# A 4096 matmul by Strassen's products on one core: the first product of five regions taken in quarters as well

## The chip, the cores and the metric

The kernel runs on one core of a Trainium2 chip. The metric is device time in microseconds (us). The kernel before took 1525.79 us (median of 3 runs, 1524.71 to 1526.01).

A core has a matrix engine (TensorE, "PE" in the profile, with its weight loads as "PEld"), a vector engine (VectorE, "DVE"), a scalar engine (ScalarE, "ACT"), GpSimd ("POOL") and a queueing engine (SyncE, "SP"). Each runs its own list of instructions in the order in which the program issued them, and waits where an operand is not there yet or a buffer is not free. TensorE accumulates into PSUM, eight banks of 128 x 512 float32. DMAs are issued from the lists of SP, ACT and POOL.

## The reference

```python
def reference(a, b, alpha):          # a, b: 4096 x 4096 float32, alpha = 0.01
    x = np.matmul(a, b)
    return np.where(x > 0, x, alpha * x)
```

## The kernel before

**Regions and products.** The output is cut into 4 row groups g of 1024 rows and 4 pairs j of 1024 columns: 16 regions (g, j). A region's output is a 2 x 2 block matrix of 512 x 512 blocks, and it is computed by Strassen's scheme in Winograd's form: seven block products instead of eight. A = (a11 a12; a21 a22) and B = (b11 b12; b21 b22) are the halves of the group's rows and the pair's columns, split along the inner dimension of 4096 into 2048 + 2048. Of A come the sums s1 = a21 + a22, s2 = s1 - a11, s3 = a11 - a21, s4 = a12 - s2; of B the sums t3 = b22 - b12, t2 = t3 + b11, t1 = b22 - t2 (the code writes it over t2) and t4 = b21 - t2. `PRODUCTS` names the order: 0 is a11 b11, 1 is a12 b21, 2 is s2 t2, 3 is s3 t3, 4 is s1 t1, 5 is a22 t4, 6 is s4 b22. In the regular regions the order of the work is 0, 1, 2, then "fifth" (s1 t1), "fourth" (s3 t3), "sixth" (a22 t4) and "seventh" (s4 b22). Everything is float16 in SBUF; whether that is allowed for the given numbers is judged at the end from measurements of squares (`Measure`, `judge`); another path stands ready if not.

**Whole products and quarters.** A whole product is 64 matmuls of 512 columns (two inner halves k, 8 chunks c, 4 row tiles mt), issued in `product` at line 831, one bank for each row tile. A product "in quarters" applies the seven-product scheme once more to the 512 x 512 blocks: seven quarter products of 16 matmuls of 256 columns (`quarter_product`, line 770), from quarter sums of both operands. In a "chain" one bank collects three of them, and ScalarE copies the running sum into other banks as their seed at the right moment.

**Which regions do what.** The first region (0, 0) has its own code; the other 15 are the loop over `regions`. In group 0 all products are whole. In groups 1 to 3 the order of pairs is 2, 0, 3, 1 (in group 3: 2, 0, 1, 3). The first of a group (pair 2) has products 0 to 4 whole and sixth and seventh in quarters. The last of groups 1 and 2 is "turning": it loads the next group's rows, and only its fourth product is in quarters. The other seven are regular (`in_fourth`): products 0, 1, 2 whole, the other four in quarters. The set `FIFTH` holds just these seven.

**Buffers.** Banks 0 to 3 and 4 to 7 change places as `y` and `z` from region to region. Product 0 ends in `y`, is copied to `z` (line 1132) as the seed of product 1, and stays in `y` as that of product 2. The results wait in tiles `c` (two pools, `side` and `1 - side`, two tiles each); `leave` applies the leaky factor (line 313, VectorE) and stores them (line 1076, SP), a store for each row tile. Quarter sums live in three buffers `a16` and in a tile `x` of four quarters (`t`). Those of S1, of a22 and of s4 are made once a group and kept in DRAM (`kept_q`), from where each region loads them (`load_sums`, line 762). s2 is kept in DRAM too and loaded anew in each region (`load_s2`).

**B.** Blocks of B come through POOL's queue, which casts them to float16 (line 547). Pair 2 of group 0 leaves a float16 copy in DRAM, pair 2 of group 1 its t3 and t2 (`kept_t`), which groups 2 and 3 load in place of b12 and the sums. Pairs 0, 1 and 3 leave b21 and b22 (`kept_half`, loaded at line 544).

**Order on VectorE in a regular region.** The seventh product's adds (lines 1005, 1009, 1011) and two leaky passes; in the second region of a group s3's second and S1's quarter sums (line 719); t3 and t2 for both k (line 603); a measurement if one is due (`EARLY`, `MEASURED`; its squares are ScalarE's, line 231); the leaky passes of product 1; t4 = b21 - t2 for both k; t1 for the first k, a quarter sum of t3 (line 696); t1 for the second k in two column halves (line 1225), which wait for the end of product 2, since they overwrite t2; then the quarter sums of the fifth product (lines 696 to 706).

Of the kernel before, what the change touches and what calls it, by code (L numbers as in the profile page):

```python
# [8 lines left out]
P = 128  # L9
# [28 lines left out]
OTHERS = (0, 3)  # L38

# [9 lines left out]
def kernel(  # L49
# [149 lines left out]

    def plain(t):  # L200
        return t.rearrange("p c m e -> p (c m e)").rearrange("p (c m) -> p c m", c=KC)
# [14 lines left out]
    class Measure:  # L216
# [21 lines left out]
        def end(self):  # L238
            total, *more = self.held
            nc.vector.tensor_add(total, total, more[0])  # L240
            self.square(3)
# [215 lines left out]
    for i in range(1, len(steps)):  # L457
# [50 lines left out]
        if i == 6:  # L508
            first_measure.end()

# [3 lines left out]
    kept_t = {name: dram_pool.tile([2, P, KC * NT], DT, name=f"kept_{name}") for name in ("t3", "t2")}  # L514
# [12 lines left out]
    def move_t(name, t, k, out, queue=nc.sync):  # L527
        ends = kept_t[name][k], t.rearrange("p c n -> p (c n)")
        queue.dma_start(*(ends if out else ends[::-1]))

    def fetch_unit(i, u, nt, later=False):
# [7 lines left out]
        if g > 1 and j == CACHED and (half, nt) == (0, 1):  # L539
            move_t("t3", t, u, False)  # L540
# [89 lines left out]
    def judge(line):  # L630
# [29 lines left out]
        (1, 3): [B11], (2, 0): [B21], (2, 3): [B21], (2, 1): [B12], (3, 1): [B11, B21],  # L660
# [15 lines left out]
    FIFTH = {(1, 0), (1, 3), (2, 0), (2, 3), (3, 0), (3, 1), (3, 3)}  # L676
# [123 lines left out]
    in_quarters = False  # L800
    for i, (g, j) in enumerate(regions):
# [6 lines left out]
        ybank = 0 if i % 2 == 0 else 4  # L808
        zbank = 4 - ybank
# [6 lines left out]
        def product(n, banks, first):  # L816
            name, half, nt = PRODUCTS[n]

# [5 lines left out]
            elif n == 1 or n == 4 and in_fourth:  # L824
# [15 lines left out]

        def keep(banks, side):
            pairs, kept = new_c(side)
            for mt in range(MT):
                nc.scalar.copy(kept[mt], banks[mt])  # L844
            return pairs, kept

# [51 lines left out]
        def fifth_in_quarters(y, banks, tq, sx, pairs, between):  # L898
# [6 lines left out]
            onto = lambda r, n: [y[2 * r + m][:, n * HALF:(n + 1) * HALF] for m in range(2)]  # L905
# [6 lines left out]
            def more(r, n, room):  # L912
                for m, to in enumerate(onto(r, n)):
                    nc.vector.tensor_add(to, to, room[:, m])

            quarter_product(x[0, 1], b[1, 0], onto(0, 0))
            quarter_product(x[0, 0], b[0, 0], into(chain), True)
            one = copied(0, 0, chain)
            quarter_product(a_quarter(sx[4]), b[1, 1], onto(0, 1))
# [3 lines left out]
            quarter_product(x[1, 1], t(4), onto(1, 0))  # L923
# [9 lines left out]
            last = copied(1, 1, chain)  # L933
            for m in range(2):
# [3 lines left out]
        def sixth_in_quarters(pairs, banks, v_pairs, v, y, tq, sq):  # L938
# [20 lines left out]
            add(v, y)  # L959
# [28 lines left out]
        def seventh_in_quarters(y, one, other, tq, sq):  # L988
# [7 lines left out]
            onto = lambda r, n: [y[2 * r + m][:, n * HALF:(n + 1) * HALF] for m in range(2)]  # L996
            quarter_product(x[0, 1], b[1, 0], onto(0, 0))
            quarter_product(x[0, 0], b[0, 0], into(one), True)
            nc.scalar.copy(block(0, 0), pair(one))
            quarter_product(sx(4), b[1, 1], onto(0, 1))  # L1000
            quarter_product(x[1, 1], t(4), onto(1, 0))
            quarter_product(sx(2), t(2), into(one))
            nc.scalar.copy(block(0, 1), pair(one))
            quarter_product(sx(1), t(1), into(other), True)
            nc.vector.tensor_add(block(0, 1), pair(other), block(0, 1))
# [4 lines left out]
            for mt in range(MT):  # L1010
                nc.vector.tensor_add(kept[mt], y[mt], kept[mt])
            return pairs

        def seventh_at_the_end(y, one, other, tq, sq, one_more):
# [9 lines left out]
            onto = lambda r, n: [part(y[2 * r + m], n) for m in range(2)]  # L1024
# [8 lines left out]
            for mt in (2, 3):  # L1033
                nc.scalar.copy(part(kept[mt], 1), part(y[mt], 1))
            quarter_product(x[0, 1], b[1, 0], onto(0, 0))
            for mt in range(2):
                more(mt, 0, part(y[mt], 0))
# [7 lines left out]
            quarter_product(sx(4), b[1, 1], onto(0, 1))  # L1045
            for mt in range(2):
                more(mt, 1, part(y[mt], 1))
# [7 lines left out]
            quarter_product(x[1, 1], t(4), onto(1, 0), by_row=True)  # L1055
            for mt in (2, 3):
                more(mt, 0, part(y[mt], 0))
# [12 lines left out]
        def leave(pairs, h, nt, some=(0, 1)):  # L1070
            for r, t in enumerate(pairs):
# [3 lines left out]
                for m in range(2):  # L1075
                    nc.sync.dma_start(place(g, h, 2 * r + m, j, nt), t[:, m, :])  # L1076
# [34 lines left out]
        y = [new_bank(ybank + mt) for mt in range(MT)]  # L1111
        z = [new_bank(zbank + mt) for mt in range(MT)]
# [6 lines left out]
        in_fifth = (g, j) in FIFTH  # L1119
        second_of_group = in_fourth and regions[i - 2][0] != g  # L1120
        early = [measure(i, *block) for block in EARLY.get((g, j), [])]
        for m in early[:1]:
# [3 lines left out]
        product(0, y, True)  # L1126
        if second_of_group:
            sums_of_s3(g, (2,))
        for m in early[:1]:
            m.end()  # L1130
        for mt in range(MT):
            nc.scalar.copy(z[mt], y[mt])  # L1132
        if second_of_group and g in [of for of, _ in FIFTH]:
            sums_of_a(g, "s1", new_a16)
        for m in early[1:]:
            m.begin()
        have_t2 = g > 1 and j == CACHED
        if have_t2:
            for k in ks:
                t = have_b[i, k, 0] = b_pool.tile([P, KC, NT], DT, name="b", tag="b11")  # L1140
                move_t("t2", t, k, False, nc.scalar)
        if middle:
            middle.begin()
        for k in ks:
            if have_t2:
                break
# [4 lines left out]
            if g == 1 and j == CACHED:  # L1151
                move_t("t3", B(0, 1, k), k, True)
                move_t("t2", B(0, 0, k), k, True)
        if middle:
            middle.end()
        for m in early[1:]:
# [23 lines left out]
        if in_fourth:  # L1180
            for k in ks:
                b_sum(B(1, 0, k), B(1, 0, k), B(0, 0, k), SUB)
# [17 lines left out]
        if in_fifth:  # L1200
# [8 lines left out]
        if in_fifth:  # L1209
# [6 lines left out]
        for k in ks:  # L1216
            halves_of = [slice(None)]
            if in_fifth and k == ks[1]:
# [256 lines left out]
```

## Time and profile before

| | |
|---|---|
| median of 3 runs | 1525.79 us |
| the profiled execution | 1526.13 us, of which the instructions span 1524.2 us |
| TensorE busy | 1512.9 us (99%) |
| VectorE busy | 1166.7 us (77%) |
| ScalarE busy | 512.2 us (34%) |
| GpSimd busy | 258.3 us (17%) |
| moved by DMA | 372.29 MB, mean 244 GB/s |

How to read the rows in this document: times are in us from the start of the span unless a row says ns. "L831" is line 831 of the kernel. A row of the chain has a start, a duration, and what ran. A row of the timeline has a start, a duration, the engine, line, operation, output<-input, the count, and in brackets the engine's idle time before it and what ended that. A row of waits names who waited for whom, the total, how often and the longest. A row of a table by stage has the stretch, its length, the busy time of PE, PEld, DVE, ACT and POOL, the granted clock, the busy share of the DMA engines and their GB/s. A row of a group has line, engine, operation, operands and count, then total busy time and the mean in ns, then idle time before and its cause. Matmuls are pipelined, so a single matmul's duration in a row is longer than the step from one to the next.

### The profile page before, as it was taken

How to read it: one execution, taken by the hardware profiler on the slowest of the kernel's cores; microseconds unless marked ns; L12 is line 12 of the kernel's file. 1: busy time of each engine (PE TensorE's matmuls, PEld its weight loads, DVE VectorE, ACT ScalarE, POOL GpSimd, SP SyncE). 2: the span in 40 equal slices, each digit the busy share in tenths (PEclk: the TensorE clock that was granted, in tenths of full speed). 3: DMA queues.
4: the chain of work that ended last, by engine and by line, in shares of the span. 5: the costliest groups of instructions: out<-in, count | busy, mean ns of one | idle time of the engine just before them, and what ended most of it. 6: DMA issues, size and time to landing. Idle time of an engine off the chain costs nothing.

```text
span 1524.2 us, 22803 instructions
## 1 busy us (share of the span) xinstructions
PE 1512.9 (99%) x9003; PEld 879.2 (58%) x9003; DVE 1166.7 (77%) x1221; ACT 512.2 (34%) x885; POOL 258.3 (17%) x426
## 2 busy tenths in 40 slices
PE   9999999999999999999999999999999999999998
PEld 4444444444446577584544748667554475848667
DVE  4588867666896597777779598777978779888797
ACT  2411535537410123124661132323574113252221
POOL 5641110233202011012320101000331100101000
PEclk9999999999999999999999999999999999999999
DMA  9999995999889999999898968859999894968935
GB/s 247 189 215 206 242 285 164 174 187 193 235 330 247 285 300 288 290 289 271 199 273 317 287 252 187 312 151 330 220 239 313 223 337 148 276 238 205 331 122 172
DMA packets 197767, 372.29 MB, mean 244 GB/s; under 512 B 19345, under 2 KB 132241, under 8 KB 184594
## 3 DMA queue, kind: packets, MB, share of 16 engines
q0 software_dynamic: 119808, 112.22, 46.7%
q1 hardware_dynamic: 71218, 232.95, 41.0%
q10 hardware_dynamic: 6624, 25.56, 4.3%
q8 instruction: 72, 1.18, 0.3%
q14 instruction: 45, 0.37, 0.1%
HBM read 359.66 MB, written 121.11 MB: 315 GB/s over the span
## 4 chain that ended last, share of the span: by engine, by line
PE 58%; DMA 6%; DVE 1%; issue 1%; SPq 0%; POOL 0%; DVEq 0%; POOLq 0%
PE ps L831 34%; PE ps L770 25%; DMA b<-in_b_dram 5%; DMA q<-kept_qs 1%; DVE b L603 0%; DVE c L313 0%; DVE c L1028 0%; POOL b L547 0%; SPq L1076 0%; DVE b L696 0%; DVE b L1225 0%; SPq L762 0%; DVEq L603 0%; DVEq L313 0%; POOLq L547 0%
## 5 line engine op out<-in xcount | busy, mean ns | idle before, releaser
L831 PE MATMUL ps<-b,a 128*128 128x512 f16 x2624 | 570.6, 379 | 0.0
L831 PEld LDWEIGHTS <-a 128*128 128x128 f16 x2624 | 256.7, 98 | 307.8
L831 PE MATMUL ps<-b,s 128*128 128x512 f16 x1792 | 391.3, 379 | 0.0
L831 PEld LDWEIGHTS <-s 128*128 128x128 f16 x1792 | 175.4, 98 | 210.9
L603 DVE TENSOR_TENSOR b<-b 128x4096 f16<-128x4096 f16 x97 | 218.9, 2286 | 51.3 <-DMA b<-in_b_dram 33.1
L547 POOL DMA_DIRECT2D b<-in_b_dram x128 | 94.8, 745 | 870.5 <-PE ps L770 266.1
L770 PEld LDWEIGHTS <-q 128*128 128x128 f16 x1872 | 182.6, 98 | 23.2 <-DMA q<-kept_qs 1.6
L844 ACT COPY c<-ps 128x512 f32<-128x512 f32 x164 | 85.9, 596 | 287.5 <-PE ps L831 277.7
L133 POOL DMA_DIRECT2D a<-in_a_dram x252 | 137.5, 553 | 246.5 <-ACT junk L622 81.3
L142 DVE STREAM_TRANSPOSE a<-a 128x512 uint32<-128x512 uint32 (+2 forms) x120 | 127.0, 1107 | 66.5 <-DMA a<-in_a_dram 66.5
L313 DVE SCALAR_TENSOR_TENSOR c<-c 128x1024 f32<-128x1024 f32 (+2 forms) x123 | 141.9, 1196 | 17.7 <-ACT c L844 17.4
L622 ACT ACTIVATE junk<-a 128x512 bf16<-128x512 f16 x192 | 121.2, 631 | 72.8 <-DMA a<-in_a_dram 67.7
L770 PEld LDWEIGHTS <-a 128*128 128x128 f16 x1200 | 117.4, 98 | 14.7
L231 ACT ACTIVATE sq<-b 128x2048 bf16<-128x2048 f16 x60 | 111.3, 1911 | 43.1 <-DVE sq L240 36.7
L770 PE MATMUL ps<-b,q 128*128 128x256 f16 x1008 | 118.6, 273 | 0.0
L283 PE MATMUL ps<-b,a 128*128 128x512 f16 x512 | 112.2, 379 | 0.5 <-ACT a L380 0.2
L770 PEld LDWEIGHTS <-s 128*128 128x128 f16 x960 | 93.8, 98 | 14.2 <-DVE b L603 1.3
L770 PE MATMUL ps<-q,q 128*128 128x256 f16 x864 | 99.9, 273 | 0.9 <-DMA q<-kept_qs 0.9
L770 PE MATMUL ps<-b,a 128*128 128x256 f16 x752 | 88.3, 273 | 0.0
L283 PEld LDWEIGHTS <-a 128*128 128x128 f16 x512 | 49.7, 98 | 60.8 <-issue 1.4
L1132 ACT COPY ps<-ps 128x512 f32<-128x512 f32 x60 | 32.8, 572 | 147.8 <-PE ps L831 147.8
L1063 DVE TENSOR_TENSOR c<-ps,c 128x512 f32<-128x512 f32 x72 | 44.6, 683 | 47.6 <-PE ps L831 38.0
(125 smaller groups left out, 1053.6 us busy)
## 6 DMA issues: line engine op xcount, KB each, us to landing
b<-in_b_dram POOLq DMA_DIRECT2D x136, 512.0 KB, 12.4
out_dram<-c SPq DMA_DIRECT2D x240, 256.0 KB, 7.8
a<-in_a_dram POOLq DMA_DIRECT2D x244, 128.0 KB, 5.7
b<-kept_half SPq DMA_DIRECT2D x28, 1024.0 KB, 11.8
b<-kept SPq DMA_DIRECT2D x20, 1024.0 KB, 9.2
q<-kept_qs ACTq DMA_DIRECT2D x40, 512.0 KB, 7.2
s<-kept_s SPq DMA_DIRECT2D x18, 1024.0 KB, 9.1
q<-kept_qs SPq DMA_DIRECT2D x28, 512.0 KB, 6.1
```

The lines of the kernel that those rows point to most:

```text
L133: nc.gpsimd.dma_start(a16[32 * q:32 * q + 32], src.rearrange("(g i) w -> i g w", i=32))
L142: nc.vector.transpose(part.rearrange("p c m e -> p c (m e)").bitcast(U32) .rearrange("p c (g i) -> p g c i", i=32), src[:, :, i * n:(i + 1 ...
L231: nc.scalar.activation(to, self.parts[n], SQUARE)
L283: nc.tensor.matmul(ps, a_cols(at[0, h, u], c, mt, (h, u) == (0, 0)), bt[0, u, nt][:, c, :], start=first, stop=last,)
L313: nc.vector.scalar_tensor_tensor(t, t, alpha, t, op0=MULT, op1=MAX if alpha <= 1 else MIN)
L547: nc.gpsimd.dma_start(t[:, c:c + 4, :], b_rows(j, u, c, 4, nt, g > 0))
L603: nc.vector.tensor_tensor(f(to), f(x0), f(x1), op)
L622: nc.scalar.activation(junk, piece[:, q, :], SQUARE, accum_out=to[:, 4 * n + q:4 * n + q + 1])
L770: nc.tensor.matmul(to[m], xq[:, c // 2, rows, c % 2], yq[:, c, :], start=first and c == 0 and m < banks, stop=c == KC - 1, skip_group_chec ...
L831: nc.tensor.matmul(banks[mt], a_cols(t, c, mt, t is first_a), B(half, nt, k)[:, c, :], start=first and (k, c) == todo[0], stop=(k, c) == t ...
L844: nc.scalar.copy(kept[mt], banks[mt])
L1063: nc.vector.tensor_add(to, bank, to)
```

## The change

**First product in quarters.** In the five regular regions of groups 2 and 3, the new set `FIRST`, product 0 is run by `first_in_quarters`: seven quarter products. The quarter sums of a11 and of the next region's b11 are made by VectorE in pieces between the steps of the seventh product of the region before (`for_the_first`), in buffers that this product has just read. The fourth sum of b11 is made inside the new function, which also copies the seeds to `z` on ScalarE and takes half a `c` tile as `room` for the quarter that two results share.

**Layout.** In these regions a bank holds a quarter of the block (256 rows by 256 columns) rather than a row tile; `onto`, `pieces` and `add_pieces` translate. `product` then runs products 1 and 2 in matmuls of 256 columns, by quarters 0, 1, 3, 2 in each k. The banks change roles by the lists `Y` and `Z`. s2's first load is issued after the first product instead of at the end of the region before.

**b21 and T1.** In all regular regions t4 for the second k is taken off the early place and made in two column halves around T1's: before them in groups 2 and 3, in turn with them in group 1, where t3's quarter sum goes behind. `FIFTH` is gone, since it held all regular regions.

**Measurements.** b21 of pair 0 is squared in the first region (`last_columns`) and not in (2, 0); b11 of pair 1 in (1, 1) and not in (3, 1). In the `FIRST` regions a measurement begins after the first product.

**Copies of B's sums.** Pairs 0 and 3 also leave t3 and t2 in DRAM, in group 2, and group 3 loads them. `leave` stores two row tiles with one DMA.

The core of the diff:

```diff
+KEPT_T = {CACHED: 1, 0: 2, 3: 2}
         if i == 6:
             first_measure.end()
+            last_columns = Measure(1, halves(bt[0, 2, 0]) + halves(bt[0, 3, 0]), False, c_rooms)
+            last_columns.begin()
+            last_columns.square(3)
...
-        if g > 1 and j == CACHED and (half, nt) == (0, 1):
-            move_t("t3", t, u, False)
+        if g > KEPT_T.get(j, G) and (half, nt) == (0, 1):
+            move_t("t3", j, t, u, False)
...
-        (1, 3): [B11], (2, 0): [B21], (2, 3): [B21], (2, 1): [B12], (3, 1): [B11, B21],
+        (1, 3): [B11], (1, 1): [B11], (2, 3): [B21], (2, 1): [B12], (3, 1): [B21],
...
+    FIRST = {(2, 0), (2, 3), (3, 0), (3, 1), (3, 3)}
...
+        if in_first:
+            shared_bank = Z[1]
+            Y, Z = [Z[2], Z[3], Y[0], Z[0]], [Y[1], Y[2], Z[1], Y[3]]
+        else:
+            Y, Z = Z, Y
...
+            if in_first:                       # in product()
+                for k in ks:
+                    for q in (0, 1, 3, 2):
+                        for c in range(KC):
+                            for m, to in enumerate(into(banks[q])):
+                                nc.tensor.matmul(
+                                    to, a_cols(operand(g, name, k), c, q // 2 * 2 + m),
+                                    B(half, nt, k)[:, c, q % 2 * HALF:(q % 2 + 1) * HALF],
...
+        def for_the_first(tq, sq, first_t, first_s):
+            first_s[1] = new_a16()
+            tt(fx(1), x1[1, 0], x1[1, 1], ADD)
+            yield
+            first_s[2] = tq[4]
+            tt(fx(2), fx(1), x1[0, 0], SUB)
+            yield
+            first_t[3], first_t[2] = new_a16(), tq[2]
+            tt(f(3), y1[1, 1], y1[0, 1], SUB)
+            tt(f(2), f(3), y1[0, 0], ADD)
+            yield
+            first_t[1], first_s[3] = new_a16(), tq[1]
+            tt(f(1), y1[1, 1], f(2), SUB)
+            tt(fx(3), x1[0, 0], x1[1, 0], SUB)
+            yield
+            first_s[4] = sq[3]
+            tt(fx(4), x1[0, 1], fx(2), SUB)
+            yield
+
+        def first_in_quarters(y, shared, z, tq, sq):
+            room = new_c(side)[0][1][:, :, :HALF]
+            one, other, third, chain = y
+            quarter_product(x[0, 0], b[0, 0], into(chain), True)
+            nc.scalar.copy(one, chain)
+            quarter_product(sx(1), t(1), into(shared), True)
+            nc.scalar.copy(room, pair(shared))
+            tq[4] = new_a16()
+            nc.vector.tensor_tensor(t(4), b[1, 0], t(2), SUB)
+            quarter_product(sx(2), t(2), into(chain))
+            nc.scalar.copy(other, chain)
+            quarter_product(x[0, 1], b[1, 0], into(one))
+            nc.scalar.copy(z[0], one)
+            quarter_product(sx(3), t(3), into(chain))
+            nc.scalar.copy(third, chain)
+            nc.vector.tensor_add(pair(chain), pair(chain), room)
+            quarter_product(sx(4), b[1, 1], into(other))
+            nc.vector.tensor_add(pair(other), pair(other), room)
+            quarter_product(x[1, 1], t(4), into(third))
+            z[2] = new_bank(Z[2])
+            for to, bank in ((3, chain), (1, other), (2, third)):
+                nc.scalar.copy(z[to], bank)
...
-                for m in range(2):
-                    nc.sync.dma_start(place(g, h, 2 * r + m, j, nt), t[:, m, :])
+                nc.sync.dma_start(places(g, h, 2 * r, j, nt), t)
...
+        if in_first:
+            shared = new_bank(shared_bank)
+            first_in_quarters(y, shared, z, first_t, first_s)
+            new_s(g, "s2")
+            load_s2(g, ks[0])
+        else:
+            product(0, y, True)
...
         if in_fourth:
-            for k in ks:
-                b_sum(B(1, 0, k), B(1, 0, k), B(0, 0, k), SUB)
+            b_sum(B(1, 0, ks[0]), B(1, 0, ks[0]), B(0, 0, ks[0]), SUB)
...
+            b_sum(B(0, 0, ks[0]), B(1, 1, ks[0]), B(0, 0, ks[0]), SUB)
+            if g == 1:
+                parts = [x for both in zip(less_t2, into_t1) for x in both]
+            else:
+                parts = less_t2 + into_t1
+            for n, part in enumerate(parts):
+                if n == 2 and g > 1:
+                    t3_of_b(y7)
+                nc.vector.tensor_tensor(*part, SUB)
...
+                between = for_the_first(tq, sq, first_t, first_s) if next_first else nothing()
+                kept_c = seventh_in_quarters(*rest, between)
```

`less_t2` are the two column halves of b21 - t2 for the second k, `into_t1` those of b22 - t2 written over t2. In `seventh_in_quarters` the five pieces are drawn after its third, fourth, fifth and sixth quarter product and before its last adds.

More of the change, by code (lines that the diff above doesn't have):

```diff
@@ L933, in fifth_in_quarters @@
             last = copied(1, 1, chain)
+            if in_first:
+                more(1, 0, last)
+                more(1, 1, last)
+                return
             for m in range(2):
@@ L1118 @@
         in_fourth = in_quarters and not first_of_group
-        in_fifth = (g, j) in FIFTH
+        next_first = not final and regions[i + 1] in FIRST
         second_of_group = in_fourth and regions[i - 2][0] != g
         early = [measure(i, *block) for block in EARLY.get((g, j), [])]
-        for m in early[:1]:
+        have_t2 = g > KEPT_T.get(j, G)
+        at_once, afterwards = ([], early) if in_first or have_t2 else (early[:1], early[1:])
+        for m in at_once:
             m.begin()
@@ L1150 @@
             b_sum(B(0, 0, k), B(0, 1, k), B(0, 0, k), ADD)
-            if g == 1 and j == CACHED:
-                move_t("t3", B(0, 1, k), k, True)
-                move_t("t2", B(0, 0, k), k, True)
+            if g == KEPT_T.get(j):
+                move_t("t3", j, B(0, 1, k), k, True)
+                move_t("t2", j, B(0, 0, k), k, True)
         if middle:
             middle.end()
-        for m in early[1:]:
+        if i == 0:
+            last_columns.end()
+        for m in [] if have_t2 else afterwards:
             m.end()
```

229 lines of the change are left out of this document (127 added, 102 removed).

## The prediction

> **What bounds the kernel now.** I read the page first: busy times, then the chain that ended last in order of time, then who TensorE waited for, then the tables by stage, and last VectorE's, ScalarE's and the stores' timelines around one region's end.
>
> From the page and the chain:
>
> ```profile
> span 1524.2 us, 22803 instructions
> PE 1512.9 (99%) x9003; PEld 879.2 (58%) x9003; DVE 1166.7 (77%) x1221; ACT 512.2 (34%) x885; POOL 258.3 (17%) x426
> ...
> 876.75 41.44 PE ps L831 x192
> 918.19 48.91 PE ps L770 x448
> 967.10 41.44 PE ps L831 x192
> ...
> 1098.88 12.23 PE ps L770 x112
> ...
> 1246.07 41.44 PE ps L831 x192
> ...
> 1336.42 41.44 PE ps L831 x192
> ...
> 1426.76 41.44 PE ps L831 x192
> ```
>
> From 876.75 on the chain is TensorE and nothing else. One regular region is 41.44 us of three whole products (192 matmuls of 512 columns, line 831), then 48.91 us of four products in quarters (448 matmuls of 256 columns, line 770). The five rows at L831 from 876.75, 967.10, 1246.07, 1336.42 and 1426.76 are the five regions of the change: (2,0), (2,3), (3,0), (3,1), (3,3). TensorE waits almost nowhere:
>
> ```profile
> PE ps L770 <- DMA q<-kept_qs: 0.9, 1, 0.9
> PE ps L770 <- DVE b L1225: 0.6, 2, 0.3
> PE ps L770 <- DVE b L603: 0.6, 1, 0.6
> ```
>
> So whatever shortens TensorE's own work shortens the kernel, until another engine is late. By stage (four of the five regions), the columns being PE, PEld, DVE, ACT, POOL busy, clock, DMA share, GB/s:
>
> ```profile
> 876.75:967.10 90.35, 90.35 (x641) 62.55 (x640) 76.18 (x80) 24.08 (x34) 5.92 (x8) 1.00 0.79 239
> 967.10:1057.44 90.34, 90.34 (x641) 62.59 (x640) 69.28 (x74) 24.13 (x34) 5.92 (x8) 1.00 0.80 239
> 1246.07:1336.42 90.35, 90.35 (x641) 62.56 (x640) 76.18 (x80) 24.11 (x34) 5.92 (x8) 1.00 0.80 240
> 1336.42:1426.76 90.34, 90.34 (x641) 62.58 (x640) 75.37 (x84) 31.45 (x38) 5.92 (x8) 1.00 0.81 240
> ```
>
> The granted clock is 1.00, and VectorE has 14 to 21 us free in 90.
>
> **Part 1, TensorE's own work.** A whole product is 41.44 / 3 = 13.81 us (64 matmuls of 0.2158); seven quarter products are 12.23 us (112 of 0.1092, the row at 1098.88). The first product in quarters saves 13.81 - 12.23 = 1.58 us, five times: -7.9. But in the same regions `product` now runs products 1 and 2 in halves of 256 columns, because the seeds lie by quarters: 128 x 48.91 / 448 = 13.97 us in place of 13.81, +0.16 for each of ten: +1.6. Net -6.3 us. The weight loads double with it:
>
> ```profile
> L770 PEld LDWEIGHTS <-q 128*128 128x128 f16 x1872 | 182.6, 98 | 23.2 <-DMA q<-kept_qs 1.6
> ```
>
> 98 ns fits behind the 109 ns of one matmul, and the rate of 109 was measured with one load each, so they cost nothing more. Were they exposed, a quarter matmul would be 98 + 109 = 207 ns. The Trainium skill speaks against the edit here ("TensorE: Matmul & The Clock Gate", Back-to-back issue gap): in a stream of loads and matmuls it gives about 131 ns at 512 columns and 81 ns at 128. By estimate from these, 98 ns at 256, the whole product would be 64 x 131 = 8.4 us and the quarters 112 x 98 = 11.0, and five regions would lose 13 us: some 1539. The rows say 215.8 and 109.2 and so decide against it.
>
> **Part 2, VectorE's added sums.** Costs of one sum, from the timeline inside (2,0):
>
> ```profile
> 921.88 1.23 DVE L702 TENSOR_TENSOR q<-b 128x2048 f16<-128x2048 f16 x1
> 923.14 1.23 DVE L704 TENSOR_TENSOR q<-b,q 128x2048 f16<-128x2048 f16 x1
> 924.28 1.22 DVE L706 TENSOR_TENSOR q<-b,q 128x2048 f16<-128x2048 f16 x1
> ...
> 883.80:890.95 7.15, 7.15 (x35) 3.24 (x34) 6.23 (x12) 3.50 (x5) 0.00 (x0) 1.00 0.46 175
> ...
> L603 DVE TENSOR_TENSOR b<-b 128x4096 f16<-128x4096 f16 x97 | 218.9, 2286 | 51.3 <-DMA b<-in_b_dram 33.1
> ```
>
> The fourth row is the stretch of one measurement's sums in (2,0) (VectorE 6.2 us), the last the whole-block sums of B (2.29 each). Each first product needs four sums of a11, and three and one of b11: 8 x 1.22 = 9.8, and two adds in PSUM, 1.4 (0.69 each, below): +11.2 us a region. Taken away: one measurement (6.2) each in (2,0) and (3,1), and in (3,0) and (3,3) the four sums T3 and T2, which are loaded (4 x 2.29 = 9.2). VectorE goes to about 81 of 89 us in (2,0) (76.2 + 11.2 - 6.2), 80 in (2,3) and (3,1), 78 in (3,0). It fits in sum, so the order decides. The end of (2,0), E = 967.10, VectorE and ScalarE:
>
> ```profile
> 957.34 2.36 DVE L313 SCALAR_TENSOR_TENSOR c<-c 128x1024 f32<-128x1024 f32 x2
> 965.44 0.69 DVE L1005 TENSOR_TENSOR c<-ps,c 128x512 f32<-128x512 f32 x1 [5.74 <-issue]
> 967.75 0.69 DVE L1009 TENSOR_TENSOR c<-ps,c 128x512 f32<-128x512 f32 x1 [1.61 <-ACT c L1008]
> 968.36 2.47 DVE L1011 TENSOR_TENSOR c<-ps,c 128x512 f32<-128x512 f32 x4
> 970.75 2.35 DVE L313 SCALAR_TENSOR_TENSOR c<-c 128x1024 f32<-128x1024 f32 x2
> ...
> 967.13 1.07 ACT L1008 COPY c<-ps 128x512 f32<-128x512 f32 x2 [2.91 <-PE ps L770]
> ```
>
> There are 5.7 idle us before E. Each new sum takes a buffer that a quarter product of the seventh has just read; a quarter takes 12.23 / 7 = 1.75, so they can start at E-6.9, -5.1, -3.4, and T3, T2, T1 (1.26 apart where one reads the other, else 1.14) reach E+0.3. T1 and S1 are wanted at E+1.75: in time. The next sum, the two adds of lines 1005 and 1009, the last sum, four adds and two leaky passes then stand in a row: about E+1.4, 2.0, 2.6, 3.8, 6.2, 8.5, and T4 is ready at E+9.7. Its quarter starts at 6 x 1.75 = E+10.5: 0.8 to spare, no cost. The seed copy into the seventh's old bank waits for line 1009's add: E+2.7, copied by 3.4, wanted at 3.5. I allow 0.05 a region, 0.2 in all.
>
> **Part 3, a wait that comes in: ScalarE behind the stores.** The shared quarter is copied into a `c` tile (`room`) at E+3.5. That tile's last holder is the sixth product's result, which must have left first. At the ends of (2,0) and of (3,0) its last store is this:
>
> ```profile
> L1076 SPq DMA_DIRECT2D out_dram<-c x1: 332/332/332, 963.4 to 963.4; - x1
> DMA to landing us min/median/max: 10.1/10.1/10.1
> ...
> L1076 SPq DMA_DIRECT2D out_dram<-c x1: 332/332/332, 1332.8 to 1332.8; - x1
> DMA to landing us min/median/max: 10.5/10.5/10.5
> ...
> 949.00:973.00 24.00, 24.00 (x195) 18.83 (x194) 16.64 (x21) 7.61 (x8) 0.00 (x0) 1.00 1.09 342
> ```
>
> The first lands at 973.5 = E+6.4, the second at 1343.3 = E+6.9, with the DMA engines full (share 1.09), so issuing it sooner as one store of a pair gains little. Behind that wait, in ScalarE's order, stands the copy that frees `chain` for the fifth quarter, wanted at E+6.99. Two copies (1.07) after E+6.5 and E+7.0 it is free at 7.6 and 8.1: +0.6 and +1.1 us. What fills the engines is POOL's load of the next B12:
>
> ```profile
> L547 POOL DMA_DIRECT2D b<-in_b_dram x2: 742/746/750, 941.2 to 941.9; - x2
> DMA to landing us min/median/max: 24.9/27.9/30.9
> ```
>
> Issued at 941.9, it lands 30.9 us later, at E+5.7. Ahead of (2,0) and (3,0) the previous region loads it a product earlier, ahead of (3,3) 2 MB of T3 take its place: I take nothing at these three. Were all five like (3,0), it would be 5.5, were the stores on time, 0.
>
> **Part 4, T1 in (3,0).** Here T1 had no slack already:
>
> ```profile
> 1260.09 1.23 DVE L719 TENSOR_TENSOR q<-s,q 128x2048 f16<-128x2048 f16 x1 [3.35 <-DMA kept_qs<-q]
> 1261.35 5.51 ACT L231 ACTIVATE sq<-b 128x2048 bf16<-128x2048 f16 x3 [0.59 <-DVE q L719]
> 1287.55 2.36 DVE L1225 TENSOR_TENSOR b<-b 128x2048 f16<-128x2048 f16 x2
> ```
>
> T1's halves began at 1287.55, as product 2 ended (1246.07 + 41.44 = 1287.51). The fourth S1 sum began at E+14.0, behind a store, and the squares 1.3 later, in the buffers that such stores free. Now T4, the PSUM adds and S3's sum come first (9.7, 11.2, 12.4), so I put the fourth sum at E+18.3, the squares at E+19.6 and 1.9 apart with each freed buffer, the last after a first add, done at E+27.4, and the fold's remaining 3.9 at E+31.3. Then leaky, b21 - t2 and T1 of the first block, 2.3 each, two halves and T3, 3.5, and half of T1, 1.2: E+42.9, wanted at 12.23 + 27.95 + 1.75 = E+41.9. I take +0.9 us; between 0 (the four T sums that stood here are gone) and 2. The other four regions come out 1 us or more early: (2,0) has no measurement left, the others no S1 sums.
>
> **Part 5, the rest.** In (2,0) and (2,3) T3 and T2 are written out, 4 MB on SP's queue ahead of S1's quarter loads. (1,0) and (1,3) write as much at the same place, with B still loading, and in (1,3) TensorE waited once for such a load:
>
> ```profile
> 644.28 1.92 PE L770 MATMUL ps<-q,q 128*128 128x256 f16 x16 [0.87 <-DMA q<-kept_qs]
> ...
> 626.00:642.00 16.00, 15.76 (x92) 8.69 (x90) 15.86 (x11) 2.76 (x5) 0.00 (x0) 1.00 1.01 413
> ```
>
> There the engines moved 413 GB/s, which makes 4.19 MB 10.2 us. In (2,0) and (2,3) the load of B is over by E+6. I take 0 (up to 10.2 us each: rival C). In row group 1, T1 comes a sum sooner, but the quarter loads land no sooner: 0, at best -1.5 (the waits above). b21 of pair 0 is squared and folded in group 0, which shows no wait of TensorE; the 6.2 us of VectorE there stand ahead of S3's sum, some 1 us short of its product by my reckoning: 0, up to +1. (1,1) gets the measurement that (2,1) has with no wait: 0. T2's loads on ScalarE's queue go out as they do for pair 2: 0. Merged stores: fewer issues on SP, off the path.
>
> **Sum.** -7.9 + 1.6 + 0.2 + 0.6 + 1.1 + 0.9 = -3.5 us. The profiled execution took 1526.13 (span 1524.2 and 1.9 around it), 0.34 above the median: 1522.6, or 1522.3 against the median.
>
> **The rivals.** (A) Nothing new is late: the stores land by E+4 and T1 by E+41.9. For it: 0.8 us and more of slack elsewhere; against: the two landings. -6.3, with row group 1's waits -7.8: 1518 to 1519.5. (B) VectorE's row of work after E is longer than reckoned, and T4 is late: it has 0.8 us, so 1.9 too many (a sum and an add) make 1.1 us at the three ends where nothing else is waited for, +3.3 on the forecast: 1525.6, no change. (C) Slower: the 4 MB that (2,0) and (2,3) write. They could push S1's quarters, wanted 3.5 us into the fifth product, behind them. Half of the 10.2 us exposed in both regions is +10: 1532. It decides for slower from 3.3 us in each (3.5 + 3.05 = 6.6). For it: (1,3)'s wait of 0.9; against: the writes start some 20 us before the loads are wanted. (D) Time goes by instructions, not columns: weight loads exposed, 207 ns a quarter matmul, 112 x 0.207 = 23.2 us in place of 13.8, +47: 1573. The Trainium skill's figures above are the mild form of it. The 448 quarter matmuls in 48.91 us leave it next to nothing.
>
> **How the numbers follow.** A difference of 0.2% (3.05 us) is about what a measurement of this kernel can tell. Forecast 0.45, A 0.27, B 0.16, C 0.11, D 0.01. The forecast's own range, 1520.5 to 1524.5, straddles 1522.74: two thirds of it counts as faster, 0.30. Faster 0.27 + 0.30 = 0.57, same 0.15 + 0.16 = 0.31, slower 0.12. The range runs from A with half of row group 1's waits (1518.7) to B and a start of C (1528).
>
> **What would show it.** In the changed profile's chain, the three whole products of the five regions become 12.23 and 27.95 us, all on line 770 and the line of `product`. Part 3 right: ScalarE's copy of the shared quarter waits for a store at the starts of (2,3) and (3,1), TensorE 0.5 to 1.1 us behind it. Part 4 right: TensorE waits for T1 in (3,0) alone. Waits for `kept_qs` loads in (2,0) or (2,3) would be C, waits for T4 at all five starts B. I am wrong on the size if waits sum to more than 3 us or less than 2.

## The result, and the profile after

The changed kernel took 1528.33 us (median of 15 runs, 1526.83 to 1531.74) beside 1525.60 us (15 runs, 1524.12 to 1526.73) for the kernel before: a ratio of 1.0019, 95% interval 1.0012 to 1.0027. The forecast was 1522.3 with a range to 1528.0; the time is 0.3 us outside it, on the slower side. The profiled execution took 1528.09 us with a span of 1526.3, 2.1 longer than before.

The chain that ended last, after (start, duration, what ran):

```profile
...
1290.72 1.15 DVE b L1351
1291.87 0.04 issue
1291.91 61.27 PE ps L781 x544
1353.18 27.95 PE ps L839 x256
1381.12 61.19 PE ps L781 x560
1442.31 27.95 PE ps L839 x256
1470.26 49.02 PE ps L781 x448
```

L781 is a quarter product, L839 `product` in 256 columns. From one L839 row to the next is the length of a region: 1442.31 - 1353.18 = 89.13 us, where a region took 41.44 + 48.91 = 90.35. So the quarters give what they promised. But TensorE's work at 1291.91 did not follow on its own work: it had just waited for VectorE's T1 (L1351). TensorE's waits, after, over the whole execution:

```profile
PE ps L781 <- DVE b L614: 3.1, 1, 3.1
PE ps L781 <- DVE b L1351: 2.6, 1, 2.6
...
PE ps L781 <- DMA q<-kept_qs: 1.1, 1, 1.1
PE ps L781 <- DVE q L713: 1.1, 1, 1.1
...
PE ps L858 <- DVE b L614: 0.4, 1, 0.4
```

The first two are both in (3,0), for the two blocks of T1. By the first matmul of each region, (2,0), (2,3), (3,1) and (3,3) became 1.08, 1.22, 1.21 and 1.22 us shorter, 4.73 in all, and (3,0) 6.60 longer. Group 0 lost 0.6 and group 1 won 0.5 back; (2,0) starts at 876.77, before at 876.59. Together that is 0.18 - 4.73 + 6.60 = +2.05, the whole difference between the two profiled executions (the medians differ by 2.73). What has to be explained is in (3,0). Below, E is the start of a region's first matmul, here E = 1243.79; the prediction takes it from the chain, which reads 0.16 us later. VectorE in (3,0):

```profile
1256.39 1.22 DVE L730 TENSOR_TENSOR q<-s 128x2048 f16<-128x2048 f16 x1
...
1258.79 1.22 DVE L730 TENSOR_TENSOR q<-s 128x2048 f16<-128x2048 f16 x1
1267.48 1.22 DVE L730 TENSOR_TENSOR q<-s,q 128x2048 f16<-128x2048 f16 x1 [7.48 <-DMA kept_qs<-q]
...
1272.88 1.23 DVE L246 TENSOR_TENSOR sq<-sq 128x2048 bf16<-128x2048 bf16 x1 [4.16 <-ACT sq L237]
...
1280.38 2.35 DVE L320 SCALAR_TENSOR_TENSOR c<-c 128x1024 f32<-128x1024 f32 x2
1282.65 4.67 DVE L614 TENSOR_TENSOR b<-b 128x4096 f16<-128x4096 f16 x2
1287.23 2.35 DVE L1351 TENSOR_TENSOR b<-b 128x2048 f16<-128x2048 f16 x2
```

L730 are the S1 sums, L246 the first add of b22's measurement (with the adds behind it, up to the leaky pass, it is called the fold), L320 leaky, L614 b21 - t2 and T1 of the first k, L1351 the column halves. The fourth S1 sum stood 7.48 us in front of a buffer that the first sum's store had to free. It started at E+23.7 (forecast E+18.3), the fold ended at E+36.6 (forecast 31.3). In the same kernel the DMA issues from 1254 to 1266, queue rows with packets, MB and share of the engines, then issues with the median time to landing:

```profile
q10 hardware_dynamic: 274, 2.05, 49.2%
q1 hardware_dynamic: 513, 2.02, 44.9%
...
b<-kept_t ACTq DMA_DIRECT2D x2, 1024.0 KB, 8.5
kept_qs<-q SPq DMA_DIRECT2D x3, 512.0 KB, 10.0
```

T2's load, 2 MB on ScalarE's queue (q10), took half of the engines' time just when SP (q1) had the S1 stores: 10.0 us from issue to landing, in the kernel before 5.6.

### The profile page after: what moved, and what is told of

It reads as the page before. It is cut to its first block, busy times and chain, and to the rows that moved or that the text cites. A ratio compares the mean times of both kernels' runs of the same rounds, so it can differ in the third digit from the quotient of the medians.

```text
span 1526.3 us, 24424 instructions
## 1 busy us (share of the span) xinstructions
PE 1508.6 (99%) x9883; PEld 966.2 (63%) x9883; DVE 1201.3 (79%) x1250; ACT 523.8 (34%) x905; POOL 252.2 (17%) x418
## 3 DMA queue, kind: packets, MB, share of 16 engines
q1 hardware_dynamic: 71058, 245.53, 42.9%
## 5 line engine op out<-in xcount | busy, mean ns | idle before, releaser
L858 PE MATMUL ps<-b,a 128*128 128x512 f16 x1984 | 431.6, 379 | 0.0
L858 PEld LDWEIGHTS <-a 128*128 128x128 f16 x1984 | 194.1, 98 | 233.2
L858 PE MATMUL ps<-b,s 128*128 128x512 f16 x1472 | 321.5, 379 | 0.4 <-DVE b L614 0.4
L858 PEld LDWEIGHTS <-s 128*128 128x128 f16 x1472 | 143.9, 98 | 173.9 <-DVE b L614 0.9
L781 PEld LDWEIGHTS <-q 128*128 128x128 f16 x2192 | 214.3, 98 | 28.5 <-DMA q<-kept_qs 2.8
L614 DVE TENSOR_TENSOR b<-b 128x4096 f16<-128x4096 f16 x82 | 185.8, 2285 | 43.6 <-DMA b<-in_b_dram 37.8
L781 PEld LDWEIGHTS <-a 128*128 128x128 f16 x1440 | 140.9, 98 | 17.4
L320 DVE SCALAR_TENSOR_TENSOR c<-c 128x1024 f32<-128x1024 f32 (+2 forms) x123 | 141.7, 1191 | 5.4 <-ACT c L881 5.1
L781 PE MATMUL ps<-b,q 128*128 128x256 f16 x1088 | 128.4, 273 | 1.1 <-DMA q<-kept_qs 1.1
L781 PE MATMUL ps<-q,q 128*128 128x256 f16 x1024 | 119.0, 273 | 1.1 <-DVE q L713 1.1
L290 PE MATMUL ps<-b,a 128*128 128x512 f16 x512 | 112.2, 379 | 0.3
L781 PE MATMUL ps<-b,a 128*128 128x256 f16 x912 | 107.4, 273 | 0.0
L781 PEld LDWEIGHTS <-s 128*128 128x128 f16 x960 | 94.5, 99 | 18.0 <-DVE b L614 3.3
L290 PEld LDWEIGHTS <-a 128*128 128x128 f16 x512 | 49.7, 98 | 60.7 <-issue 1.4
L839 PE MATMUL ps<-b,a 128*128 128x256 f16 x640 | 70.7, 273 | 0.0
L839 PE MATMUL ps<-b,s 128*128 128x256 f16 x640 | 70.7, 273 | 0.0
```

Source lines behind the costliest of these rows:

```text
L290: nc.tensor.matmul(ps, a_cols(at[0, h, u], c, mt, (h, u) == (0, 0)), bt[0, u, nt][:, c, :], start=first, stop=last,)
L320: nc.vector.scalar_tensor_tensor(t, t, alpha, t, op0=MULT, op1=MAX if alpha <= 1 else MIN)
L614: nc.vector.tensor_tensor(f(to), f(x0), f(x1), op)
L781: nc.tensor.matmul(to[m], xq[:, c // 2, rows, c % 2], yq[:, c, :], start=first and c == 0 and m < banks, stop=c == KC - 1, skip_group_chec ...
L839: nc.tensor.matmul(to, a_cols(operand(g, name, k), c, q // 2 * 2 + m), B(half, nt, k)[:, c, q % 2 * HALF:(q % 2 + 1) * HALF], start=False, ...
L858: nc.tensor.matmul(banks[mt], a_cols(t, c, mt, t is first_a), B(half, nt, k)[:, c, :], start=first and (k, c) == todo[0], stop=(k, c) == t ...
```

## The experiments

All edits are to the changed kernel (some with t2_behind's edit as well, where it is said), and each is compared with the kernel before on the same chip. The theory was that in (3,0) S1's sums, their stores, b22's squares and the fold form one row ahead of T1, made longer by T2's load.

**no_measure: the row without its end.**

```diff
-        (3, 0): (B22, [], None, None), (3, 3): (B22, [], None, None),
+        (3, 3): (B22, [], None, None),
```

> The measurement of b22 in (3,0) is left out, so the judgement on float16 lacks that block; all products are computed. Theory (in (3,0) the S1 sums, the stores that free their buffers, the squares and the fold stand in a row ahead of T1, and that row is some 5 us longer than the prediction had it): without squares and fold T1 is ready before product 2 ends, TensorE waits in (3,0) for nothing, the granted clock stays at 1.00 there, and region (3,0) becomes 1.2 us shorter than in the kernel before rather than 6.8 longer: about 8 us less than the changed kernel, 1520.5. Rival (T1 is late for another reason, T2's load or the order on VectorE): the waits of 3.2 and 2.8 us stay within 1 us and the time stays at 1527 to 1528.

Measured: 1522.04 us, ratio 0.9976 (0.9962 to 0.9990). TensorE waited for nothing from 1240 to 1330, and the granted clock stayed at 1.00. The median is 1.5 above the expected value (the kernel before, too, was 1.2 slower in this comparison than in the result above). The fourth S1 sum was as late as ever (7.48 us in front of the store), so lateness of the sums alone costs nothing: it costs through what stands behind them.

**t2_behind: the load out of the way.** T2 is issued on SP, behind the four S1 stores.

```diff
-                move_t("t2", j, t, k, False, nc.scalar)
+                move_t("t2", j, t, k, False, nc.sync if second_of_group else nc.scalar)
```

> In (3,0) the two loads of T2 (2 MB) are issued on SP behind the stores of the four S1 sums, and not on ScalarE's list ahead of them. Theory (the stores took 9.8 to 10.3 us because T2's load and s2's load shared the engines with them): the stores land 3 to 6 us after issue, the fourth S1 sum starts near E+19 instead of E+23.7, the fold ends near E+32 instead of E+36.7, TensorE's wait for T1 is under 1.5 us in all and the clock does not drop: 1520.5 to 1522. Rival (the sums are late because the first product's own sums hold VectorE; the store times do not matter): fold still after E+35, time within 1 us of the changed kernel's 1528.

Measured: 1522.12 us, ratio 0.9972 (0.9962 to 0.9983). The DMA issues from 1254 to 1266, then VectorE, then the chain:

```profile
kept_qs<-q SPq DMA_DIRECT2D x4, 512.0 KB, 3.1
b<-kept_t SPq DMA_DIRECT2D x2, 1024.0 KB, 7.5
```
```profile
1262.73 1.23 DVE L730 TENSOR_TENSOR q<-s,q 128x2048 f16<-128x2048 f16 x1 [0.75 <-DMA kept_qs<-q]
...
1275.70 2.35 DVE L320 SCALAR_TENSOR_TENSOR c<-c 128x1024 f32<-128x1024 f32 x2
...
1286.32 2.36 DVE L1351 TENSOR_TENSOR b<-b 128x2048 f16<-128x2048 f16 x2 [0.26 <-PE ps L839]
```
```profile
1258.34 27.95 PE ps L839 x256
...
1347.48 27.95 PE ps L839 x256
```

The stores take 3.1 us. Here E is 1245.77, so the fourth sum is at E+17.0, the fold ends at E+29.9, and T1's halves wait for product 2 rather than the reverse. From product 1 of (3,0) to product 1 of (3,1) it takes 1347.48 - 1258.34 = 89.14 us like the other regions, 7.7 less than in the changed kernel (96.82). The choice of queue and place for one load moved the change from 0.2% slower to 0.3% faster. The rival falls.

**whole_first: no quarters in (3,0).**

```diff
-    FIRST = {(2, 0), (2, 3), (3, 0), (3, 1), (3, 3)}
+    FIRST = {(2, 0), (2, 3), (3, 1), (3, 3)}
```

> (3,0) alone has its first product whole again, with products 1 and 2 in 512 columns; T2 is still loaded there. Theory (quarters in (3,0) move the S1 sums later, and T2's loads are cheap where the sums come early): (3,0) then takes as long as in the kernel before, the other four regions keep their 1.26 us each, group 1 its 0.5: about 1525.6 - 5.5 = 1520 to 1521.5, no wait for T1 in (3,0). Rival (T2's load by itself makes T1 late, whatever the first product is): waits of 2 us and more in (3,0) stay, 1523 to 1527.

Measured: 1522.35 us, ratio 0.9976 (0.9967 to 0.9985). T2 is still loaded on ScalarE's queue, but three of the S1 sums are done before it is issued and their stores take 5.1 us; in (3,0) TensorE loses 0.5 us in all beyond its steady steps. So neither the load nor the quarters do it alone: it takes the sums moved into the load's time.

**none_first: no quarters anywhere.**

```diff
-    FIRST = {(2, 0), (2, 3), (3, 0), (3, 1), (3, 3)}
+    FIRST = set()
```

> No region has its first product in quarters; all other parts of the change stay (copies of T3 and T2 for pairs 0 and 3, T1 between the halves of t4, the measurements where the change has them, merged stores). Theory (quarters give 1.26 us in each of five regions and the rest nothing): 1525 to 1526, within 0.1% of the kernel before. Rival (the rest gains or loses by itself): if the copies of T3 and T2 or the new measurement in the first region cost time of their own, 1527 or more; if T1 between the halves gains in group 1, 1524 or less.

Measured: 1526.83 us, ratio 1.0003 (0.9994 to 1.0012); the kernel before had 1526.75 in the same comparison. What the change does beside the quarters comes to nothing in sum.

**t2_summed: no copies of T3 and T2 for pair 0.**

```diff
-KEPT_T = {CACHED: 1, 0: 2, 3: 2}
+KEPT_T = {CACHED: 1, 3: 2}
```

> Pair 0 leaves no copies of T3 and T2 in group 2, and (3,0) makes them by VectorE as in the kernel before; the first product stays in quarters. Theory (T1 in (3,0) has next to no slack, so that 9.2 us of sums are as bad as the stores that T2's load holds up): the S1 stores land 3 to 6 us after issue and the squares start near E+20, but the four sums stand ahead of the fold, which ends near E+37, T1's halves come near E+48 and TensorE waits 4 to 7 us: 1526 to 1529, as the changed kernel. Rival (T2's load alone made T1 late; VectorE has room for its sums): waits under 1 us and 1520.5 to 1522.

Measured: 1528.46 us, ratio 1.0010 (0.9999 to 1.0021). Its VectorE and TensorE in (3,0):

```profile
1265.43 1.23 DVE L730 TENSOR_TENSOR q<-s,q 128x2048 f16<-128x2048 f16 x1 [0.91 <-DMA kept_qs<-q]
```
```profile
1289.74 1.92 PE L781 MATMUL ps<-b,s 128*128 128x256 f16 x16 [0.92 <-DVE b L614]
1294.28 2.88 PE L781 MATMUL ps<-b,s 128*128 128x256 f16 x16 [2.62 <-DVE b L1351]
```

The stores are quick again, but the four sums (9.1 us) stand ahead of the fold and TensorE waits 3.5 us for T1; with the slow clock behind it, (3,0) loses 5.5 us. So the copies are worth having, and it was the place of their load that was wrong. The fold ended at E+34.3, sooner than the expected E+37. The median alone would not show this: the runs go from 1524.03 to 1530.71 us, the profile is of the slowest, and 4.3 us of its time are lost in (0,1), in code that this edit leaves as it was.

**late_half: b21 of pair 0 measured in (2,0) again.**

```diff
-            last_columns = Measure(1, halves(bt[0, 2, 0]) + halves(bt[0, 3, 0]), False, c_rooms)
-            last_columns.begin()
-            last_columns.square(3)
...
-        if i == 0:
-            last_columns.end()
...
-        (1, 3): [B11], (1, 1): [B11], (2, 3): [B21], (2, 1): [B12], (3, 1): [B21],
+        (1, 3): [B11], (1, 1): [B11], (2, 0): [B21], (2, 3): [B21], (2, 1): [B12], (3, 1): [B21],
```

> b21 of pair 0 is measured in (2,0) again and not in the first region. Theory (in the second region of a group the S1 sums, a measurement and the sums T3 and T2 do not fit ahead of T1 once the first product is in quarters): TensorE waits 3 to 7 us for T1 in (2,0), and the 0.6 us of (0,1) go: 1530 to 1535. Rival (that measurement could have stayed, the changed kernel's only cost is in (3,0)): no wait in (2,0), 1527.5 to 1528.

Measured: 1533.18 us, ratio 1.0053 (1.0036 to 1.0070), 4.9 us above the changed kernel. In (2,0):

```profile
918.55 1.92 PE L778 MATMUL ps<-b,s 128*128 128x256 f16 x16 [0.90 <-DVE b L611]
923.09 2.35 PE L778 MATMUL ps<-b,s 128*128 128x256 f16 x16 [2.62 <-DVE b L1346]
```

(2,0) takes 5.5 us longer than in the changed kernel. So moving this measurement into group 0 saves some 5 us and was paid there with 0.6 us in the changed kernel's profile: it is a part of the change that the quarters cannot do without. What it costs in group 0 varies: the wait for T1 in (0,1) was 0 to 2.4 us in the ten profiles that have the same code there.

**half_later: the waits of group 1.** With t2_behind, b22's copies in (1,0) and (1,3) go out behind S1's quarter loads.

```diff
         if g == 1 and j in OTHERS:
-            keep_half()
+            keep_half((0,))
...
             load_sums("s1", s5, (3,))
+            if g == 1 and j in OTHERS:
+                keep_half((1,))
```

> T2's loads behind the S1 stores as in the run before, and in (1,0) and (1,3) the copies of b22 (2 of the 4 MB written there) are issued behind S1's quarter loads, not ahead of b21 - t2. Theory (the waits of 1.9 and 1.2 us for S1's quarters in these two regions come from the writes ahead of them): the loads land in 5 to 8 us rather than 10.6 to 12.3, both waits fall below 0.5, 1519.5 to 1520.5. Rival (the loads are issued late, or T2's quarter sum is as late as they are): less than 0.7 us gained, 1521.5 to 1522.5.

Measured: 1520.52 us, ratio 0.9965 (0.9952 to 0.9978). The loads of S1's quarters in (1,0) landed after 6.1 us (median) instead of 10.6. TensorE's waits from 530 to 660 of t2_behind, then of half_later:

```profile
PE ps L781 <- DMA q<-kept_qs: 1.8, 1, 1.8
PE ps L781 <- DVE q L713: 1.1, 1, 1.1
```
```profile
PE ps L781 <- DVE q L713: 2.2, 2, 1.1
```

The wait for the load goes and one for T2's quarter sum (L713) stands in its place, as the rival had it: of 2.9 us of waits 2.2 stay. The intervals of the two ratios overlap, so the times do not tell this run from t2_behind; 1520.52 is at the upper edge of the theory's range.

**t4_early: T1 no longer between the halves.** With t2_behind, the second k's b21 - t2 goes back to its early place. T3's quarter sum then stands ahead of T1's halves in all groups (lines not shown).

```diff
         if in_fourth:
-            b_sum(B(1, 0, ks[0]), B(1, 0, ks[0]), B(0, 0, ks[0]), SUB)
+            for k in ks:
+                b_sum(B(1, 0, k), B(1, 0, k), B(0, 0, k), SUB)
...
-            if g == 1:
-                parts = [x for both in zip(less_t2, into_t1) for x in both]
-            else:
-                parts = less_t2 + into_t1
+            parts = into_t1
```

> T2's loads behind the S1 stores as before, and b21 - t2 of the second k made early again, ahead of T1's first block, as in the kernel before, in all regular regions. Theory (T1 between the halves gives only what group 1 shows): TensorE waits about 0.5 us more in (1,0) and (1,3) together, nothing in groups 2 and 3, 1522 to 1523. Rival (the order carries T1 in (3,0) as well, where it now has some 2 us to spare): a wait for T1's first block of 1 us or more in (3,0), 1523.5 to 1525.

Measured: 1521.35 us, ratio 0.9969 (0.9958 to 0.9980), not to be told from t2_behind. In group 1 TensorE waited less, not more (0.6 for S1's quarters and 0.5 for T1). The expectation of half a microsecond lost was wrong: this part of the change shows no gain here.

**both, one_order and both_and_first.** The first joins half_later and t4_early. The second is half_later with the order of groups 2 and 3 in group 1, T3's quarter sum included (those lines are not shown):

```diff
-                parts = [x for both in zip(less_t2, into_t1) for x in both]
+                parts = less_t2 + into_t1
```

> The two edits of half_later (T2's loads behind the S1 stores; b22's copies behind S1's quarter loads) and the early t4 of t4_early together. Theory (two causes stand one behind the other in group 1: the loads of S1's quarters, and T2's quarter sum, which the order with T1 between the halves makes late): both waits of 1.24 us left in half_later go, new ones of 0.1 to 0.9 us for T1's first block take their place, 1519 to 1520. Rival (T1's wait takes all the place of the others): 1520.5 to 1521.5.

> half_later, with the order of groups 2 and 3 in group 1 as well: both halves of t4, then T1's halves with T3's quarter sum between. Theory (what is late in half_later is T2's quarter sum, because T3's sum stands behind four interleaved halves; here T3 comes sooner): the two waits of 1.24 us go or fall below 0.4, T1's second block may come 0.5 to 1 us late: 1518.5 to 1520. Rival (T1's second block is now 2.3 us later and TensorE waits 2 us for it in both regions): 1521 to 1523.

Measured: 1520.82 us, ratio 0.9960 (0.9947 to 0.9973), and 1521.09, ratio 0.9965 (0.9953 to 0.9978). In `both` the waits of 2.2 us in group 1 became these:

```profile
PE ps L781 <- DVE b L614: 1.2, 2, 0.7
PE ps L781 <- DVE b L1354: 0.7, 2, 0.3
PE ps L858 <- DVE b L614: 0.2, 1, 0.2
```

Here the rival was right: T1 is late in place of T2's quarter sum. In `one_order` 1.2 us of waits for T1's second block remain. Half_later, both and one_order lie within each other's intervals; each beats the kernel before, and the changed kernel's interval too.

The third issues the copies of b21 and b22 in (0,1) ahead of product 1's results:

```diff
+        if (g, j) == (0, LAST):
+            keep_half()
...
-        if (g, j) == (0, LAST):
-            keep_half()
```

> As both, and in (0,1) the four copies of b21 and b22 are issued ahead of product 1's results instead of behind them. Theory (in (0,1) TensorE waits 0.5 to 2.5 us because b21 - t2 there waits for b21's store, which is issued at 165.6 behind the leaky passes that the added fold delays): the store lands some 10 us earlier, the wait at 177 us goes, 0.5 to 1.5 us less than both. Rival (the sums themselves, not the store, are late): no difference.

Measured: 1525.93 us, ratio 0.9997 (0.9988 to 1.0006): 5 us worse than `both`. At 177 us TensorE does not wait for T1, but neither did it in the profile of `both`, and a longer wait came ahead of it. The loads of B from 118 to 127 in `both`, then in both_and_first, and there TensorE's wait:

```profile
b<-in_b_dram POOLq DMA_DIRECT2D x4, 512.0 KB, 16.7
```
```profile
b<-in_b_dram POOLq DMA_DIRECT2D x4, 512.0 KB, 20.3
```
```profile
PE ps L858 <- DVE a L584: 3.8, 1, 3.8
```

The copies now went out beside B's last loads, which landed later, VectorE's sums of B stood ahead of S3's and S4's (L584), and TensorE waited 3.8 us for those and lost 1.7 more to the clock behind the wait. It is the mistake of (3,0) once more: a transfer that nobody waits for, put beside one that somebody does.

## Why the prediction was wrong, step by step

**Part 1 was right.** Products 0, 1 and 2 took 12.23 and 27.95 us, and four regions gained 1.08 to 1.22 of the 1.26 reckoned. That answers rival D. The Trainium skill's figures ("TensorE: Matmul & The Clock Gate", Back-to-back issue gap), by which the edit would have lost 13 us, do not hold in this trace: 112 matmuls in 12.23 us are 0.109 us each. That estimate of 13 us was itself incomplete, since it left out products 1 and 2, which the change also runs in 256 columns.

**Part 2 was right.** T4 began at 1252.47 and was done at E+9.9 against E+9.7 reckoned and E+10.7 at which its quarter ran. The stall for the seed copy was 0.19 us at the starts of (2,0) and (3,0) and some 0.06 at the other three, 0.55 in all where 0.2 was allowed. Rival B did not come.

**Part 3 named a real wait and priced it too high, 1.7 us for 0.** ScalarE, after, at the starts of (2,3) (E = 966.03) and of (3,1) (E = 1340.73):

```profile
971.63 0.59 ACT L1107 COPY c<-ps 128x512 f32<-128x512 f32 x1 [2.10 <-DMA out_dram<-c]
972.11 0.59 ACT L1111 COPY ps<-ps 128x512 f32<-128x512 f32 x1
...
1344.57 0.59 ACT L1107 COPY c<-ps 128x512 f32<-128x512 f32 x1 [0.34 <-DMA out_dram<-c]
```

The copy waited for the store, until E+5.6 and E+3.8, not E+6.4 and E+6.9; the next copy was done before the fifth quarter wanted its bank. The step that failed here is "issuing it sooner as one store of a pair gains little". The merged store was issued at E-8.3 in both, where the last single store went out at E-3.7 and E-3.6. At (2,3) it took 13.9 us to land, where the single one took 10.1, and it was still 0.8 us sooner than reckoned, at (3,1) 3.1 us sooner.

**The step that failed stands in part 5: "T2's loads on ScalarE's queue go out as they do for pair 2: 0."** They do go out so, but in (3,0) they meet S1's stores, which pair 2's never do: S1's sums are made in the second region of a group, and pair 2's is the first. With that, part 4's E+18.3 for the fourth sum became E+23.7 and the rest of its row followed, 5.3 us later at the end of the fold. With the load out of the way (t2_behind) the same points came at E+17.0 and E+29.9, so that part 4's own working was on the safe side by 1.3 us. Its bound of "between 0 and 2" held only the sums' order and not the transfer.

The price of being late was also too low. Part 4 had half of T1's second block ready at E+42.9 and wanted at E+41.9; it was ready at E+48.1, some 6 us late. TensorE lost 3.23 + 2.78 us at 1287.38 and 1291.91 beyond its steady steps. After that its clock was low (last section), 1.66 us more. With the 0.19 of part 2 that is 7.86, and by the length of the region 6.60 + 1.26 = 7.86 has to be explained. Part 4 had put 0.9 us there.

**The rest of part 5.** The measurement in group 0 cost 0.6 us in this profile (given: 0, up to +1; other profiles of the same code there show more and less, see late_half). Group 1's waits, as steps of TensorE beyond the steady ones, went from 3.0 to 2.6 us (given: 0 to -1.5). (2,0) and (2,3) wrote their 4 MB at no cost, so rival C did not come.

**The rivals.** The sign was lost because the only slower case of any weight was C, and what happened is its mechanism at another place: large transfers beside small ones that somebody waits for. It was worked out for the new writes and not for the new loads. Once the load is moved, t2_behind's ratio of 0.9972 means -4.3 us, between the forecast (-3.5) and rival A (-6.3). That nearness to the forecast is luck: in its profile the five regions gained 5.8 us, close to A's 6.3, since nothing of parts 3 and 4 had to be paid, and the groups ahead of them lost 2.1, which the forecast had at nothing.

## What to carry to other kernels

List every transfer that a change adds, on whatever queue, and look up which small transfers it will be beside and who waits for those; a load that replaces a sum is not free because it is early. Where a store frees a buffer that the next step needs, issue the large load behind it in the same queue rather than beside it. A wait of some 3 us of TensorE can cost more than its length, so price waits near that with the slow clock behind them.

## What the runs showed of the hardware

**A transfer on one queue takes the time of another's.** S1's stores of 512 KB took 10.0 us beside T2's load on ScalarE's queue, 5.1 where the load came later (whole_first) and 3.1 with the load behind them. With no load of T2 at all (t2_summed) it was 3.2. In the changed kernel the engines' time stood 49.2% to 44.9% between the two queues. The Trainium skill ("DMA: Bandwidth & Descriptors", Queues, rings and completion order) says that a DMA engine takes turns between the queues it has work for, packet by packet; the near-equal shares fit that, though no row here shows the order of the packets.

**The clock fell to half behind most gaps of 2.4 us and more, and not behind every one.** Table by stage of the changed kernel (length, then busy time of PE, PEld, DVE, ACT, POOL, then the granted clock, DMA share and GB/s), and TensorE at its two waits in (3,0):

```profile
1286.00:1288.00 2.00, 0.62 (x6) 0.57 (x7) 2.00 (x2) 0.00 (x0) 0.00 (x0) 1.00 0.96 313
1288.00:1290.00 2.00, 1.30 (x12) 1.01 (x11) 2.00 (x3) 0.00 (x0) 0.00 (x0) 1.00 0.93 377
1290.00:1292.00 2.00, 0.09 (x1) 0.09 (x1) 2.00 (x3) 0.00 (x0) 0.00 (x0) 1.00 0.71 289
1292.00:1294.00 2.00, 2.00 (x12) 1.47 (x12) 1.97 (x2) 0.00 (x0) 0.00 (x0) 0.56 0.00 0
1294.00:1296.00 2.00, 2.00 (x13) 1.48 (x12) 1.93 (x3) 0.58 (x1) 0.00 (x0) 0.59 0.00 0
```
```profile
1287.38 1.92 PE L781 MATMUL ps<-b,s 128*128 128x256 f16 x16 [3.07 <-DVE b L614]
1291.91 3.31 PE L781 MATMUL ps<-b,s 128*128 128x256 f16 x16 [2.61 <-DVE b L1351]
1295.01 2.22 PE L781 MATMUL ps<-b,q 128*128 128x256 f16 x16
1297.07 1.91 PE L781 MATMUL ps<-q,q 128*128 128x256 f16 x16
```

A quarter steps in 1.75 us at full clock; behind the gap of 2.61 us it took 3.10 and then 2.06, so 1.66 us were lost. Behind the gap of 3.07 us just before, the longer one, the clock stayed full. So these rows do not tell whether the second gap did it or both together. A single gap in (0,1) of t2_summed, of 2.38 us with no other near it, was enough:

```profile
178.00:180.00 2.00, 1.16 (x3) 0.42 (x4) 2.00 (x2) 0.00 (x0) 0.74 (x1) 0.72 1.10 312
180.00:182.00 2.00, 2.00 (x6) 0.76 (x5) 2.00 (x2) 0.00 (x0) 0.00 (x0) 0.50 1.11 180
```

There 64 matmuls stepped in 15.51 us rather than 13.81, so 1.70 us were lost. In all, the drop came behind six of the seven gaps of 2.38 to 3.83 us in these profiles, and behind none of the gaps of up to 1.82 us (the longest of these is in no_measure, at 643.68). The Trainium skill ("TensorE: Matmul & The Clock Gate", Part 1) puts the half clock behind an idle window of about 3.4 us and full clock behind as long a busy one. The length of the slow stretch agrees: 1.66 and 1.70 us lost at half clock are 3.3 and 3.4 us of it. The gap needed was shorter here. Why some gaps suffice and others do not was not tried.
